# The opening of a two-layer decoder trunk: four projection tiles interleaved in chunks of k, and an identity made on the chip

## The chip, the core and the metric

The kernel runs on one core of a Trainium2 chip. A core has TensorE (matmuls; in the profile PE, and PEld for its weight loads), VectorE (DVE), ScalarE (ACT), GpSimd (POOL) and SyncE (SP, which here only issues loads and stores), each with an instruction stream of its own that runs in order. They meet through semaphores. Working memory is SBUF, with 128 partitions; matmuls write to PSUM, of which this kernel uses eight banks of 128 x 512 float32. DMA engines move data between the chip's memory and SBUF. The metric is the time of one execution on the device in microseconds, lower is better.

## The reference

Two layers of a trunk for 256 tokens of width 1024, all float32. The part that the change touches is the first feed-forward step of the first layer:

```python
D_MODEL, SEQ, DEPTH, D_FF = 1024, 256, 2, 2816

def swiglu(x, w_gate, w_up, w_down):
    return (jax.nn.silu(x @ w_gate) * (x @ w_up)) @ w_down

h = x
for l in range(DEPTH):
    h = h + 0.5 * swiglu(rms_norm(h, ffn1_norm[l]), ffn1_w_gate[l], ffn1_w_up[l], ffn1_w_down[l])
    h = h + hybrid_mixer(rms_norm(h, mix_norm[l]), ...)     # three attention groups, then w_out
    h = h + 0.5 * swiglu(rms_norm(h, ffn2_norm[l]), ffn2_w_gate[l], ffn2_w_up[l], ffn2_w_down[l])
```

`rms_norm` divides a token by the root of its mean square and multiplies by a gain for each column.

## The kernel before

**Split numbers.** Every float32 operand of a large matmul is split into a high part (the value rounded to the fast matmul type) and a low part (the rest). A product is then high x high + high x low + low x high. `norm.x` (tile `xhl`) holds both parts of the normalized, transposed activations side by side, 8 k tiles of 128 with 2 x 256 columns; `norm.h` and `norm.l` are its halves. A projection tile of 128 output columns is a wide pass (weights' high part against 512 columns, 8 matmuls) and a narrow pass (low part against 256 columns, 8 matmuls). The two halves of the PSUM bank are then added by `summed`: ScalarE copies one half to SBUF, VectorE adds the other.

**Weights.** The class `Weights` streams all weights of the program through five raw buffers of 1 MB (`RAW_BUFS`) and eight pairs of split buffers (`wh`, `wl`). A raw tile holds two units (for the feed-forward step two tiles of 128 columns with all 8 k). `high` casts a unit on ScalarE (line 117), `low` subtracts on VectorE (line 121), `take` hands a unit to the matmuls, and `pump` does one cast and one subtraction ahead of need, as long as fewer than seven units lie ready. When both units of a raw tile are split, `issue` starts the next load, on SyncE's queue. Loads, units and matmuls all keep one order, which `add_ffn` writes down when the program is built. All instruction orders are as written in the program: nothing is moved by a scheduler.

**The feed-forward loop.** `ffn` runs over 22 tiles f of 128 hidden columns. For each it needs a gate and an up projection, `gated` and `silu` (VectorE, with a tanh on ScalarE), and `hidden`, which multiplies by up, splits the result (`hh` on ScalarE, then a `W.pump`, then `hl` on VectorE) and keeps it for the down projection, which lags by four tiles (`DOWN_LAG`). The projections use four PSUM banks under the tag `gu`, in turn. From f = 6 on in the first step, and everywhere else, gate and up run as a `Pair`: for even f both wide passes, then both narrow ones; for odd f the narrow ones first (`swapped`). In the first step the tiles f < 6 (`PAIR_FROM`) run singly, first gate, then up, by `proj`; the third gate tile uses one of the other four banks (`acc`).

**The opening.** The identity for TensorE's transposes comes from memory, on ScalarE's queue (line 184), as do the gains of the first norm. SyncE loads x in four quarters of 256 columns, with the first gate tile's two k halves between them, then the first up tile, then the second halves of those two raw tiles. TensorE runs warm-up matmuls on a tile of ones (`WARM` = 7, twice). `norm.turn` transposes two k tiles of x, `first_norm` writes their high part on ScalarE (line 320) and their low part on VectorE (line 323), and `gate` starts the first gate tile on them while the next quarter arrives, in three passes of 256 columns. For this first tile the cast is on ScalarE (line 1150) and the subtraction on GpSimd (line 1151), in two halves. Then come the first up tile, the second gate tile, the sums of squares, and so on. The norm's factor (`sums`, `broadcast`) is applied after the projection, in `gated` and `silu`.

Of the kernel before, what the change touches and what calls it, by code (L numbers as in the profile page):

```python
# [18 lines left out]
P = 128  # L19
# [18 lines left out]
WARM = 7  # L38
PAIR_FROM = 6
# [102 lines left out]
def kernel(ctx: ExitStack, tc: tile.TileContext, x, ffn1_norm, ffn1_w_gate, ffn1_w_up, ffn1_w_down,  # L142
# [25 lines left out]
    cst = cp.tile([P, 640], F32, name="cst")  # L168
# [15 lines left out]
    nc.scalar.dma_start(cst[:, 0:P], const[:, 0:P])  # L184
# [18 lines left out]
    def add_ffn(wg, wu, wd, first=False):  # L203
# [3 lines left out]
        def half(kind, i):  # L207
            j = i // 2
            if (kind, j) not in rid:
                if kind == "d":  # L210
                    rid[kind, j] = W.add_raw((2, D), [(np.s_[:], dsrc[:, 2 * j:2 * j + 2, :])])
                else:
                    src = gsrc if kind == "g" else usrc
                    src = src[:, :, 256 * j:256 * j + 256]
                    cuts = [np.s_[:]]
                    if first and j == 0:
                        cuts = [np.s_[:, :, 0:P], np.s_[:, :, P:2 * P]]
                        if kind == "g":
                            cuts[:1] = [np.s_[:, 0:4, 0:P], np.s_[:, 4:8, 0:P]]
                    rid[kind, j] = W.add_raw((KT, 256), [(c, src[c]) for c in cuts])  # L220
            o = i % 2
            if kind == "d":
                W.add_unit(rid[kind, j], lambda r, o=o: r[:, o:o + 1, :], D, 1)
            else:
                W.add_unit(rid[kind, j], lambda r, o=o: r[:, :, o * P:(o + 1) * P], D, KT)

        for f in range(NF):
            half("g", f)
            if not first or f >= PAIR_FROM:
                half("u", f)  # L230
# [4 lines left out]
            if first and f < PAIR_FROM:  # L235
                half("u", f)
# [35 lines left out]
    nc.sync.dma_start(cst[:, P:], const[:, P:])  # L272
# [7 lines left out]
    ident = cst[:, 0:128]  # L280
    tri = cst[:, 128:256]
    future = cst[:, 256:384]
    cs = cst[:, 384:640].rearrange("p (t c) -> p t c", t=2)
# [90 lines left out]
    def ffn(norm, nxt, aside=None, g0=None):  # L374
# [23 lines left out]
        def proj(between=None, after=0, tag="gu"):  # L398


            w = W.take()
            ps = bank(tag).rearrange("p (a b) -> p a b", a=2)
            for k in range(KT):
                mm(ps, w[0][:, k], norm.x[:, k], k == 0, False)
            for k in range(KT):
                mm(ps[:, 0], w[1][:, k], norm.h[:, k], False, k == KT - 1)
                if between and k == after:
                    between()
            return ps

        class Pair:


            def __init__(self):
                self.ws = [W.take() for _ in range(2)]
                self.ps = [bank("gu").rearrange("p (a b) -> p a b", a=2) for _ in range(2)]

            def wide(self, ks):
                for w, ps in zip(self.ws, self.ps):
                    for k in ks:  # L420
                        mm(ps, w[0][:, k], norm.x[:, k], k == 0, False)

            def narrow(self, ks):
                for w, ps in zip(self.ws, self.ps):
                    for k in ks:
                        mm(ps[:, 0], w[1][:, k], norm.h[:, k], False, k == KT - 1)

            def swapped(self, between):

                for w, ps in zip(self.ws, self.ps):  # L430
                    for k in range(KT):
                        mm(ps[:, 0], w[1][:, k], norm.h[:, k], k == 0, False)
                between()
                for w, ps in zip(self.ws, self.ps):
                    for k in range(KT):
                        mm(ps, w[0][:, k], norm.x[:, k], False, k == KT - 1)
# [37 lines left out]
        first = g0 is not None  # L474
        early = {}
        if first:
            u0 = proj()
            g1 = proj(norm.sums, 6)
            W.pump()
            W.low()  # L480
            g0 = summed(g0)
            u1 = proj(norm.broadcast, 6)
            W.pump(2)
            early[2] = proj(tag="acc")
        else:
            lo, hi = range(KT // 2), range(KT // 2, KT)
# [5 lines left out]
            W.pump()  # L492
            norm.sums()
            (g0, u0), (g1, u1) = p0.both(hi), p1.ps
            W.pump()
            g0, u0 = summed(g0), summed(u0)
            W.pump()
            p1.wide(hi)
            norm.broadcast()
            p1.narrow(hi)  # L500
            W.pump()
        early[1] = g1
# [3 lines left out]
        hidden(0, t_, th, summed(u0) if first else u0)  # L506
        acc = [bank("acc") for _ in range(4)]
        for f in range(1, NF):
            last = f == NF - 1
            paired = not first or f >= PAIR_FROM  # L510
            inside = paired and f > 1

# [4 lines left out]
            if not paired:  # L517
                g, u = summed(early[f] if f in early else proj()), u1 if f == 1 else None
            else:
                if f == 1:  # L520
                    g, u = g1, u1
                elif f % 2:
                    g, u = Pair().swapped(lagging)
                else:
                    p = Pair()
                    p.wide(range(KT))
                    lagging()
                    p.narrow(range(KT))
                    g, u = p.ps
                if last:  # L530
                    W.pump()
                g = summed(g)
                if not last:
                    u = summed(u)
# [4 lines left out]
            else:  # L539
                W.pump()  # L540
                if not inside:
# [4 lines left out]
            hidden(f, t_, th, u if paired and not last else summed(u or proj()), 3 if last else 1)  # L546
# [580 lines left out]
    for i in range(WARM):  # L1127
        mm(warm[:, :P], ones, ones, i == 0, i == WARM - 1)
    norm = Norm(0, 0)
    src, wh, wl = W.high_tiles()  # L1130
    g0 = bank("gu").rearrange("p (a b) -> p a b", a=2)
    xT = []

    def turn_x(mp):
        xT.append(norm.turn(mp))

    def gate(w, xs, ks):
        for k in ks:
            mm(g0[:, int(xs is norm.l)], w[:, k], xs[:, k], w is wh and xs is norm.h and k == 0,
               xs is norm.l and k == KT - 1)  # L1140

    def first_norm(mp):
        for i in range(2):
            norm.high(2 * mp + i, xT[mp][:, i])
        for i in range(2):
            norm.low(2 * mp + i, xT[mp][:, i])

    def split_gate(hf):
        ks = slice(4 * hf, 4 * hf + 4)
        A.copy(wh[:, ks], src[:, ks])  # L1150
        G.tensor_tensor(wl[:, ks], src[:, ks], wh[:, ks].bitcast(F32), op=ALU.subtract)

    turn_x(0)
    turn_gains(0)
    for i in range(WARM):
        mm(warm[:, P:2 * P], ones, ones, False, i == WARM - 1)
    split_gate(0)
    first_norm(0)
    turn_x(1)
    split_gate(1)  # L1160
    for mp in range(4):
        ks = range(2 * mp, 2 * mp + 2)
        gate(wh, norm.h, ks)
        if mp < 2:
            turn_x(mp + 2)
        if mp > 0:
            gate(wl, norm.h, range(4) if mp == 1 else ks)
        gate(wh, norm.l, ks)
        if mp < 3:
            first_norm(mp + 1)  # L1170
    W.low_done()
    W.take()
    W.high()
    W.low()
    W.high()
    W.low()
    for c in range(2):
        for t in range(2):
            norm.squares(t, c)
    W.high()  # L1180
    W.low()
    for l in range(DEPTH):
        norm = ffn(norm, lambda: Norm(1, l), lambda: before_mixer(l), g0 if l == 0 else None)
# [37 lines left out]
```

## Time and profile before

| | |
|---|---|
| median of 3 runs | 1039.59 us (1039.53 to 1040.01) |
| profiled execution | 1040.75 us, of which the span from first to last instruction is 1039.0 us |
| TensorE busy | 1032.8 us, 99% of the span, 5659 matmuls |
| VectorE, ScalarE, GpSimd busy | 78%, 57%, 14% |
| loaded | 179.67 MB, 174 GB/s over the span |
| granted TensorE clock | 1.000 of full speed |

Times in the rows are microseconds from the span's start. A row of the timeline reads: start, duration, engine, line, operation, output <- inputs, shape, count of merged instructions, and in brackets the idle time before it and what ended that. Matmuls overlap in their pipeline, so the distance between starts, not the duration, is what one costs. "SPq" and "ACTq" are issues of loads. Each landing time is counted from the start of the issue.

### The profile page before, as it was taken

Reading aid. Unit: us, or ns where it says so; the run is one execution under the profiler, and the core shown is the slowest. Engines: PE = TensorE matmul, PEld = TensorE weight load, DVE = VectorE, ACT = ScalarE, POOL = GpSimd, SP = SyncE. Lnnn points to the kernel's source line nnn. Section 1 sums busy time; section 2 is a strip of 40 time slices with the busy share of each in tenths; the row PEclk is TensorE's granted clock in tenths of the full one; section 3 lists DMA queues with packets and bytes.
Section 4 is the critical chain, followed back from the end, with each engine's and each line's share of the span. In section 5 each row is a group of like instructions: output and inputs, shape, how many; then the busy total and the mean of one; then the engine's idle time right before and its main releaser. Section 6 shows DMA issues by size and latency. Waiting matters only on the chain.

```text
span 1039.0 us, 15103 instructions
## 1 busy us (share of the span) xinstructions
PE 1032.8 (99%) x5659; PEld 899.7 (87%) x5659; DVE 807.9 (78%) x1536; ACT 593.8 (57%) x1047; POOL 142.3 (14%) x173
## 2 busy tenths in 40 slices
PE   8999999999999999999999999999999999999998
PEld 8888888898888888888888888888988988888887
DVE  4988778789876877777778777787898768777776
ACT  6655555667754655555465555557667546555552
POOL 1003000167700000000000110002765000000000
PEclk9999999999999999999999999999999999999999
DMA  9764646555441354746645564655455214555631
GB/s 292 249 226 150 240 152 226 168 184 193 144 144 42 122 205 160 242 146 220 203 163 175 198 207 158 243 177 180 163 185 180 82 61 157 189 201 165 231 133 41
DMA packets 130905, 181.70 MB, mean 175 GB/s; under 512 B 7008, under 2 KB 104720, under 8 KB 130832
## 3 DMA queue, kind: packets, MB, share of 16 engines
q1 hardware_dynamic: 130656, 180.65, 51.8%
q8 instruction: 45, 0.74, 0.3%
q14 instruction: 28, 0.23, 0.1%
q10 hardware_dynamic: 176, 0.07, 0.0%
HBM read 179.67 MB, written 1.05 MB: 174 GB/s over the span
## 4 chain that ended last, share of the span: by engine, by line
PE 99%; DMA 1%; SPq 0%; issue 0%; ACT 0%; DVE 0%; ACTq 0%
PE ps_gu L296 66%; PE ps_acc L296 30%; PE ps_acc L331 1%; PE ps_gu L980 1%; PE ps_gu L1082 1%; DMA trunk<-in_x_dram 1%; PE ps_acc L681 0%; PE ps_acc L980 0%; PE ps_gu L1013 0%; SPq L91 0%; SPq L188 0%; PE ps_acc L357 0%; PE ps_acc L1013 0%; ACT pT L982 0%; DVE trunk L370 0%
## 5 line engine op out<-in xcount | busy, mean ns | idle before, releaser
L121 DVE TENSOR_TENSOR wl<-raw,wh 128x1024 fp32r<-128x1024 f32 (+2 forms) x343 | 416.8, 1220 | 28.7 <-ACT wh L117 28.4
L117 ACT CAST wh<-raw 128x1024 fp32r<-128x1024 f32 (+2 forms) x343 | 345.5, 1036 | 6.2 <-PE ps_gu L296 4.9
L296 PE MATMUL ps_gu<-xhl,wh 128*128 128x512 f32 (+1 forms) x1408 | 329.4, 388 | 0.0
L296 PEld LDWEIGHTS ps_gu<-xhl,wh 128*128 128x128 f32 x1408 | 262.0, 188 | 52.9
L296 PEld LDWEIGHTS ps_gu<-xhl,wl 128*128 128x128 f32 x1400 | 175.8, 191 | 4.2
L296 PE MATMUL ps_gu<-xhl,wl 128*128 128x256 f32 x1400 | 178.9, 283 | 0.0
L296 PE MATMUL ps_gu<-wh,xhl 128*128 128x512 f32 (+2 forms) x512 | 158.5, 379 | 0.0
L448 DVE TENSOR_TENSOR tmp<-ps_gu,tmp 128x256 f32<-128x256 f32 x175 | 72.8, 422 | 105.2 <-ACT tmp L447 105.0
L296 PE MATMUL ps_acc<-wh,hh 128*128 128x512 f32 (+1 forms) x352 | 137.2, 390 | 0.0
L296 PE MATMUL ps_acc<-wl,hh 128*128 128x512 f32 (+1 forms) x352 | 137.0, 389 | 0.0
L296 PE MATMUL ps_acc<-wh,hl 128*128 128x512 f32 (+1 forms) x352 | 136.5, 388 | 0.0
L447 ACT COPY tmp<-ps_gu 128x256 f32<-128x256 f32 x175 | 63.4, 370 | 91.1 <-PE ps_gu L296 91.0
L296 PEld LDWEIGHTS ps_gu<-wh,xhl 128*128 128x128 f32 x512 | 94.8, 188 | 14.5
L462 ACT CAST hh<-tmp 128x256 fp32r<-128x256 f32 x80 | 32.6, 407 | 120.0 <-DVE tmp L459 120.0
L296 PE MATMUL ps_gu<-wl,xhl 128*128 128x512 f32 (+2 forms) x256 | 95.7, 374 | 0.0
L454 ACT ACTIVATE tmp<-tmp 128x256 f32<-128x256 f32 x88 | 36.9, 419 | 82.0 <-DVE tmp L452 81.7
L307 POOL TENSOR_TENSOR y_n<-msq,minus_half 128x2 f32<-128x2 f32 x6 | 6.8, 1138 | 534.6 <-DVE msq L306 534.6
L296 PEld LDWEIGHTS ps_acc<-wh,hl 128*128 128x128 f32 x352 | 66.1, 188 | 13.9
L296 PEld LDWEIGHTS ps_acc<-wh,hh 128*128 128x128 f32 x352 | 66.3, 188 | 12.5
L296 PEld LDWEIGHTS ps_acc<-wl,hh 128*128 128x128 f32 x352 | 66.3, 188 | 12.1
L296 PEld LDWEIGHTS ps_gu<-wl,xhl 128*128 128x128 f32 x256 | 48.2, 188 | 6.6
L472 DVE TENSOR_TENSOR tmp<-tmp,rb 128x256 f32<-128x256 f32 x88 | 37.5, 427 | 3.0
(221 smaller groups left out, 995.4 us busy)
## 6 DMA issues: line engine op xcount, KB each, us to landing
raw<-in_ffn_w_down_dram SPq DMA_DIRECT2D x44, 1024.0 KB, 5.0
raw<-in_ffn_w_gate_dram SPq DMA_DIRECT2D x43, 1024.0 KB, 7.0
raw<-in_ffn_w_up_dram SPq DMA_DIRECT2D x43, 1024.0 KB, 7.5
raw<-in_w_in_dram SPq DMA_DIRECT2D x24, 1024.0 KB, 5.0
raw<-in_w_out_dram SPq DMA_DIRECT2D x8, 1024.0 KB, 4.8
raw<-in_w_in_dram SPq DMA_DIRECT2D x4, 768.0 KB, 4.7
raw<-in_w_in_dram SPq DMA_DIRECT2D x4, 656.0 KB, 4.1
trunk<-in_x_dram SPq DMA_DIRECT2D x4, 256.0 KB, 5.4
```

The costliest lines, as they stand in the source:

```text
L117: self.nc.scalar.copy(hv, src)
L121: (engine or self.nc.vector).tensor_tensor(lv, self.srcs[self.n_low], hv.bitcast(F32), op=ALU.subtract)
L296: T.matmul(o, l, r, start=start, stop=stop, skip_group_check=True)
L307: G.tensor_tensor(y, dst, minus_half[:, :n], op=ALU.pow)
L331: T.transpose(ps[:, i, t * P:(t + 1) * P], trunk[:, t, (2 * mp + i) * P:(2 * mp + i + 1) * P], ident)
L447: A.copy(o, ps[:, 1])
L448: V.tensor_tensor(o, ps[:, 0], o, op=ALU.add)
L454: A.activation(th, t_, AF.Tanh, scale=0.5)
L462: (V.tensor_copy if late else A.copy)(hh, t_)
L472: V.tensor_tensor(t_, t_, norm.rb, op=ALU.mult)
L980: T.transpose(b[:, j * P:(j + 1) * P], pj[i][:, j * P:(j + 1) * P], ident)
L1082: T.transpose(b[:66, i * S + t * P:i * S + (t + 1) * P], src[t][:, 2 * hp_ + i, :], ident)
```

## The change

- The first two raw tiles (gate and up of f = 0 and 1) are loaded in three pieces each, by k: 0-1, 2-3, 4-7, all 256 columns at a time. SyncE's order is x quarter 0, gate 0-1, up 0-1, x quarter 1, gate 2-3, up 2-3, x quarters 2 and 3, gate 4-7, up 4-7, and then the third and fourth raw tile in column halves. A unit of the first two raw tiles is now four k with 256 columns.
- A new function `opening` runs the gate and up tiles of f = 0 and 1 together, in four PSUM banks. For each quarter of x it transposes, splits, and runs the wide pass of all four tiles on that k, with the narrow passes behind. In it GpSimd casts the first two pieces of both raw tiles and the last piece of the gate's, VectorE subtracts for the gate's first pieces and GpSimd for the up's. The rest of these four tiles then runs through the code that the later steps use.
- All f run as `Pair`, and the unit order is gate, up for every f. `proj` and `PAIR_FROM` are gone.
- The identity is made on GpSimd from the tile of ones. The constants are loaded in one piece, without an identity, where the rest of them was loaded before.
- The gains are transposed ahead of x, and the warm-up is 6 matmuls ahead of these transposes and 3 behind the first ones.

```diff
-WARM = 7
-PAIR_FROM = 6
+WARM = 6
+BRIDGE = 3
...
-    nc.scalar.dma_start(cst[:, 0:P], const[:, 0:P])
+    G.affine_select(out=ident, in_=ones, pattern=[[-1, P]], compare_op=ALU.is_equal, fill=0.0, base=0,
+                    channel_multiplier=1)
...
-                    if first and j == 0:
-                        cuts = [np.s_[:, :, 0:P], np.s_[:, :, P:2 * P]]
-                        if kind == "g":
-                            cuts[:1] = [np.s_[:, 0:4, 0:P], np.s_[:, 4:8, 0:P]]
+                    if first and j < 2:
+                        cuts = ([np.s_[:, 0:2], np.s_[:, 2:4], np.s_[:, 4:8]],
+                                [np.s_[:, :, 0:P], np.s_[:, :, P:2 * P]])[j]
...
+            elif first and j == 0:
+                W.add_unit(rid[kind, j], lambda r, o=o: r[:, 4 * o:4 * o + 4], D, 4)
...
         for f in range(NF):
             half("g", f)
-            if not first or f >= PAIR_FROM:
-                half("u", f)
+            half("u", f)
...
-            if first and f < PAIR_FROM:
-                half("u", f)
...
-    W.by_hand = 2
-    W.n_raw_done -= RAW_BUFS - 2
+    W.by_hand = 4
+    W.n_raw_done -= RAW_BUFS - 4
     W.issue()
-    for mp in range(1, 4):
-        if mp < 3:
-            W.load(0, mp - 1)
+    for m in range(2):
+        if m:
+            load_x(m)
+        for i in range(2):
+            W.load(i, m)
+    for mp in range(2, 4):
         load_x(mp)
-    W.load(1, 0)
-    W.load(0, 2)
-    W.load(1, 1)
-    W.n_raw_done += RAW_BUFS - 2
+    for i in range(2):
+        W.load(i, 2)
+    for m in range(2):
+        for i in range(2):
+            W.load(2 + i, m)
+    W.n_raw_done += RAW_BUFS - 4
     W.issue()
...
+        def opening():
+            low = [W.high_tiles() for _ in range(2)]
+            p0, p1 = (Pair([[[v[:, k, f * P:(f + 1) * P] for k in range(4)] for v in (h, l)] for _, h, l in low])
+                      for f in range(2))
+            def highs(m):
+                ks = slice(2 * m, 2 * m + 2)
+                for src, h, _ in low:
+                    G.tensor_copy(h[:, ks], src[:, ks])
+            def lows(m):
+                ks = slice(2 * m, 2 * m + 2)
+                for E, (src, h, l) in zip((V, G), low):
+                    E.tensor_tensor(l[:, ks], src[:, ks], h[:, ks].bitcast(F32), op=ALU.subtract)
+            def wide(k):
+                for i in range(2):
+                    for p in (p0, p1):
+                        mm(p.ps[i], p.ws[i][0][k], norm.x[:, k], k == 0, False)
+            def narrow(k):
+                for i in range(2):
+                    for p in (p0, p1):
+                        mm(p.ps[i][:, 0], p.ws[i][1][k], norm.h[:, k], False, False)
...
+            xT = norm.turn(0)
+            warm_up(BRIDGE)
+            highs(0)
+            parts(0, xT)
+            lows(0)
+            wide(0)
+            xT = norm.turn(1)
+            wide(1)
+            narrow(0)
+            narrow(1)
+            highs(1)
+            parts(1, xT)
+            lows(1)
+            for _ in range(2):
+                W.low_done()
+                W.take()
+            squares(0)
+            xT = norm.turn(2)
+            wide(2)
+            parts(2, xT)
+            xT = norm.turn(3)
+            wide(3)
+            parts(3, xT)
+            narrow(2)
+            narrow(3)
+            src, h, _ = W.high_tiles()
+            G.tensor_copy(h, src)
+            W.high()
+            W.low()
+            W.low()
+            squares(1)
...
         if first:
-            u0 = proj()
-            g1 = proj(norm.sums, 6)
-            W.pump()
-            W.low()
-            g0 = summed(g0)
-            u1 = proj(norm.broadcast, 6)
-            W.pump(2)
-            early[2] = proj(tag="acc")
+            p0, p1 = opening()
         else:
             p0, p1 = Pair(), Pair()
             p0.wide(lo)
             norm.half(1)
             p0.narrow(lo)
             p1.both(lo)
+        W.pump()
+        norm.sums()
+        (g0, u0), (g1, u1) = p0.both(hi), p1.ps
+        W.pump()
+        g0, u0 = summed(g0), summed(u0)
+        W.pump()
+        p1.wide(hi)
+        norm.broadcast()
+        p1.narrow(hi)
+        W.pump()
```

More of the change, by code (lines that the diff above doesn't have):

```diff
@@ L505, in ffn @@
         silu(t_, th)
-        hidden(0, t_, th, summed(u0) if first else u0)
+        hidden(0, t_, th, u0)
         acc = [bank("acc") for _ in range(4)]
@@ L540, in ffn @@
                 W.pump()
-                if not inside:
+                if f == 1:
                     lagging()
@@ L545, in ffn @@
             silu(t_, th)
-            hidden(f, t_, th, u if paired and not last else summed(u or proj()), 3 if last else 1)
+            hidden(f, t_, th, summed(u) if last else u, 3 if last else 1)
             if f == 8 and aside:
```

154 lines of the change are left out of this document (48 added, 106 removed).

## The prediction

> **What bounds the kernel now.** I read the page's busy shares first, then TensorE's waits over the whole run, then its timeline around the opening, and then the loads and the ScalarE/VectorE/GpSimd rows that feed it.
>
> ```profile
> span 1039.0 us, 15103 instructions
> PE 1032.8 (99%) x5659; PEld 899.7 (87%) x5659; DVE 807.9 (78%) x1536; ACT 593.8 (57%) x1047; POOL 142.3 (14%) x173
> ...
> PE ps_acc L331 <- DMA trunk<-in_x_dram: 1.7, 1, 1.7
> PE ps_gu L296 <- POOL minus_half L183: 1.0, 1, 1.0
> PE ps_gu L296 <- ACT pT L982: 0.2, 1, 0.2
> ...
> 0.97 3.35 PE L296 MATMUL ps_gu<-ones 128*128 128x128 f32 x14 [0.97 <-POOL minus_half L183]
> 4.32 0.70 PE L331 MATMUL ps_acc<-cst,trunk 128*128 128x128 f32 x4
> 4.95 0.23 PE L177 MATMUL ps_gu<-cst,tmp 16*128 16x16 f32 x1
> 5.11 1.83 PE L296 MATMUL ps_gu<-ones 128*128 128x128 f32 x14
> 6.77 0.60 PE L331 MATMUL ps_acc<-cst,trunk 128*128 128x128 f32 x4
> 7.13 0.48 PE L296 MATMUL ps_gu<-xhl,wh 128*128 128x256 f32 x2
> 9.36 0.66 PE L331 MATMUL ps_acc<-cst,trunk 128*128 128x128 f32 x4 [1.74 <-DMA trunk<-in_x_dram]
> 15.79 2.00 PE L296 MATMUL ps_gu<-xhl,wh 128*128 128x512 f32 x8
> 17.63 1.12 PE L296 MATMUL ps_gu<-xhl,wl 128*128 128x256 f32 x8
> 18.59 2.00 PE L296 MATMUL ps_gu<-xhl,wh 128*128 128x512 f32 x8
> 27.19 2.00 PE L296 MATMUL ps_gu<-xhl,wh 128*128 128x512 f32 x8
> ```
>
> TensorE has three waits in all. After 9.36 it only once waits again, for 0.2 us, so from there the time is a pile of matmuls with no slack. The opening can only help or harm by the moment at which that pile is resumed. One projection tile (eight k, a wide 512-column and a narrow 256-column pass) costs 18.59 - 15.79 = 2.80 us. Up to 9.36 the useful work was eight transposes (0.35 to 0.4 us for four: 6.77 to 7.13, and 9.36 to the next row at 9.77), the gains and two matmuls: about 1.2 us. So some 8.1 us of the start are idle or warm-up. That is all that can be won, less the 4 us until x lands.
>
> A yardstick follows. In order, six projections (gate and up of f = 0, 1, 2) are done when the seventh starts at **27.19**. The changed kernel does the same six before its seventh (the gate of f = 3, on `swapped`), and the later matmul list is the same in amount. The change in time is therefore the start of that seventh projection minus 27.19, unless a new wait comes later.
>
> **The change part by part.** *The identity.* The const load on ScalarE's queue goes and GpSimd makes the identity. The program also holds a library-load instruction on GpSimd ahead of its first work that is not a memset: before that is L1151, after it is the select, so it moves to the front of the path.
>
> ```profile
> 1.15 0.15 POOL L601 MEMSET eighth<- 128x64 f32 x1
> 5.72 1.27 POOL L1151 TENSOR_TENSOR wl<-raw,wh 128x512 fp32r<-128x512 f32 x1 [4.41 <-ACT wh L1150]
> 9.35 1.29 POOL L1151 TENSOR_TENSOR wl<-raw,wh 128x512 fp32r<-128x512 f32 x1 [2.36 <-ACT wh L1150]
> ...
> 0.72 0.20 POOL L181 MEMSET ones<- 128x128 f32 x1 [0.29 <-POOLq L1209]
> ...
> DMA to landing us min/median/max: 3.5/3.5/3.5
> 1.21 0.48 SPq L91 DMA_DIRECT2D raw<-in_ffn_w_gate_dram  x1
> DMA to landing us min/median/max: 3.8/3.8/3.8
> ```
>
> The load lies somewhere in the 4.41 us in which GpSimd was idle before 5.72, so it costs 0 to 4.4 us, and the identity is ready between 1.2 and 5.6 us. x's first quarter, issued at 0.72, landed 3.5 us later at 4.2, and the first gate piece, second in the queue before and after, at 1.21 + 3.8 = 5.0. If the load is short, the identity is early; at worst the transposes slip by 1.4 us. I take a small value and keep 1.4 us as the bound of this part. It is covered, because the seventh projection waits for something later (below). The Trainium skill ("GPSIMD Engine Reference", section "Instruction dispatch") says that the first call to a freshly loaded kernel pays about 6 us; the trace disagrees, since the first such call here ran 4.4 us after the memsets at its ordinary 1.27 us. By that page the identity would be there at 7.2 and the sum below would rise by at most 0.2 us, since GpSimd's work would end some 2.6 us later.
>
> *Four tiles together.* By rows, wide(k) is four wide matmuls (2.00 / 8 each, or 0.92 us at their spacing), so half of the four tiles (k 0 to 3) is 5.6 us of work on 512 KB of x and 1 MB of weights. It replaces nothing: it is the same matmuls sooner, and the first gate tile's three 256-column passes become 512 + 256 (gain below 0.1 us). Warm-up shrinks from 7 + 7 to 6 + 3 matmuls, in time that is idle anyway. GpSimd now does five casts, four of 128x512 and one of 128x1024, and two subtractions (1.28 us each). No row shows a GpSimd cast; it reads less than the subtraction (1.28 us) and writes more than the 0.20 us memset of 128x128 scaled to 512 columns (0.6 us): 0.6 to 1.28 us each, double for the large one. At 1.28 GpSimd, starting on the gate piece at 5.0, needs 4 x 1.28 + 2 x 1.28 + 2.56 = 10.2 us and is done at 15.2; at 0.6 it follows the loads. With the second half of the four tiles (5.6 us) plus broadcast behind 15.2, the four tiles end at about 21.1 and f = 2 (2 x 2.80) at 26.7; at the short price about 26.0. So TensorE itself would be ready for the seventh projection at 26.0 to 26.7: **0.5 to 1.2 us early**.
>
> *What is late next.* The seventh projection writes the PSUM bank of f = 1's gate, which `summed` (ScalarE copy, VectorE add) must first empty. In the changed order, on ScalarE's queue, `hidden(0)` pumps a weight cast ahead of that copy, and by the new unit order (gate and up alternating from the start) it is the cast of f = 4's up weights: the sixth raw tile, the first for which a buffer has to come free. ScalarE works in order, so the copy stands behind a transfer. Before, the cast in that place belonged to weights of an earlier raw tile.
>
> ```profile
> raw<-in_ffn_w_gate_dram SPq DMA_DIRECT2D x43, 1024.0 KB, 7.0
> ...
> trunk<-in_x_dram SPq DMA_DIRECT2D x4, 256.0 KB, 5.4
> ...
> cst<-in_const_dram SPq DMA_DIRECT2D x1, 256.0 KB, 9.3
> ...
> 20.80 0.39 SPq L91 DMA_DIRECT2D raw<-in_ffn_w_down_dram  x1
> DMA to landing us min/median/max: 7.3/7.3/7.3
> 21.29 0.41 SPq L91 DMA_DIRECT2D raw<-in_ffn_w_up_dram  x1
> DMA to landing us min/median/max: 9.5/9.5/9.5
> 2.28 0.47 SPq L91 DMA_DIRECT2D raw<-in_ffn_w_gate_dram  x1
> DMA to landing us min/median/max: 6.4/6.4/6.4
> ...
> 10.00:20.00 10.00, 10.00 (x66) 9.04 (x65) 6.94 (x12) 8.39 (x18) 1.33 (x2) 1.00 0.97 291
> 20.00:30.00 10.00, 10.00 (x62) 8.90 (x61) 7.82 (x14) 5.54 (x10) 0.00 (x0) 1.00 1.06 374
> ```
>
> The loads are in one queue and the queue is full: the DMA engines are 97 to 106% busy from 10 to 30 us (last rows, last two columns: share and GB/s). So landing follows the bytes queued ahead. Before, the first down tile had landed at 20.80 + 7.3 = 28.1, with 7,520 KB queued up to its end (x 1024, five raw tiles 5120, const 64 + 256, small ones 32, itself 1024). In the changed order the up tile of f = 4 comes in that place, with 64 KB less: **27.9** if the stream runs as before (1024 KB per 2.7 us there: 21.29 + 9.5 = 30.8 is the next). The other end: from 8.68 (2.28 + 6.4, 1,096 KB) the remaining 6,360 KB at the 374 GB/s of the last row take 17.4 us, **26.1**. The first two raw tiles now come in 1 KB rows where before had 512-byte rows, and the next two the other way round: the same mixture, so I stay nearer to the 27.9 and take 27.2.
>
> ```profile
> 27.66 1.05 ACT L117 CAST wh<-raw 128x1024 fp32r<-128x1024 f32 x1
> 28.61 0.36 ACT L447 COPY tmp<-ps_gu 128x256 f32<-128x256 f32 x1
> ...
> 29.00 0.42 DVE L448 TENSOR_TENSOR tmp<-ps_gu,tmp 128x256 f32<-128x256 f32 x1 [0.22 <-ACT tmp L447]
> ...
> 34.30 0.42 DVE L448 TENSOR_TENSOR tmp<-ps_acc,tmp 128x256 f32<-128x256 f32 x1 [0.22 <-ACT tmp L447]
> ```
>
> Behind the landing come cast, copy and add: 28.61 - 27.66 + 29.00 - 28.61 + 0.42 = 1.76, with the hand-overs about 1.85 us. Seventh projection: 27.2 + 1.85 = 29.05, against 27.19: **+1.9 us**; at the ends 27.95 (+0.8) and 29.75 (+2.6). TensorE's readiness at 26.0 to 26.7 is hidden by it, and so are the identity, the casts and the early x. What TensorE wins by starting sooner goes into this one wait of 2.4 to 3 us. After it VectorE's time for a tile, (34.30 - 29.00) / 2 = 2.65 us, fits TensorE's 2.80, as before, so I cost later waits at nothing; the later loads are then asked for 1.9 us later, too, which keeps them covered.
>
> The profiled execution took 1040.75 us, 1.75 over its span and 1.2 over the median of 1039.59. I carry the difference over to the median: 1039.6 + 1.9 = **1041.5**.
>
> **The rivals.** *The loads are in time* (one piece at 374 GB/s from 5 us on, landing before 25.3): seventh projection at 26.0 to 27.2, 1038.4 to 1039.6. For it: nothing queued early is in 512-byte rows. Against it: 291 GB/s between 10 and 20 us in a full queue.
>
> *No wait at all in the opening* (loads early and GpSimd at its short price, so that only x's landing and the transposes hold TensorE): 8.1 us of idle shrink to about 6, 1037.5. Against it: nine hand-overs between four engines in 15 us.
>
> *GpSimd becomes the bound* (the other side): if a cast takes longer than the subtraction, or VectorE's subtractions beside it slow both, GpSimd ends at 5.0 + 6c + 2.56, and the seventh projection starts 11.4 us later. It decides from 29.05 on, c = 1.7 us; at c = 2.0 it is 31.0, +3.8: 1043.4. Against it: both L1151 rows took 1.27 to 1.29 with VectorE at work on the same tiles' neighbours.
>
> *The clock falls in the gap.* TensorE then stands still for 2.4 to 3 us. The opening rows show a slow state (14 instructions in 3.35 us, later 14 in 1.83) and that a gap of 1.74 us does not bring it back; a longer one is not in this trace. If it does, about 3.4 us of work run at half speed: +1.7, 1043.2. The Trainium skill ("TensorE: Matmul & The Clock Gate", Part 1) puts that at a whole idle window of about 3.4 us; the gap is shorter, so by it the chance is small.
>
> *The identity is later than the const load was* is possible up to 5.6 us, as worked out, and changes nothing but the early idle time.
>
> **How the numbers follow.** Cases: the wait on ScalarE 0.60; loads in time 0.20; no wait 0.05; GpSimd 0.10; clock 0.05. A measurement of this kernel can tell about 0.2%, 2.1 us. The first case spans +0.8 to +2.6: 0.27 of it lies above 2.1, 0.33 below; with GpSimd and clock, slower has 0.42. Loads in time give 0.17 to same and 0.03 to faster, no wait 0.05: same 0.50, faster 0.08. The range leaves out 0.05 at the low end and the worst of the last two cases: 1038.3 to 1043.4; the likeliest case alone has 1040.4 to 1042.2.
>
> **What would show it.** In the changed profile: the first wide matmul at 6.3 to 7.5 us; the four tiles done at 20 to 21 (before: 21.5); then one wait of TensorE of 2 to 3 us before f = 3's first narrow matmul, at about 29, released by VectorE's add, with ScalarE idle before the cast of the sixth raw tile on a gate or up load that landed at about 27. I am wrong if that load lands before 25, if there is no wait between 24 and 31, or if GpSimd's casts take over 1.3 us and TensorE's waits name it.

## The result

The changed kernel took 1042.6 us (median of 9 runs, 1041.5 to 1043.88), the kernel before 1039.85 us beside it (9 runs, 1039.53 to 1040.18): the ratio is 1.0025, with an interval of 1.0016 to 1.0034. The profiled execution of the changed kernel took 1043.26 us with a span of 1041.2; TensorE is busy for 99% of it, as before. The four longest of its five waits over the whole run (the fifth is the one of 0.2 us that the kernel before has too):

```profile
PE ps_gu L300 <- DVE tmp L439: 2.1, 1, 2.1
PE ps_gu L300 <- POOL minus_half L184: 1.0, 1, 1.0
PE ps_gu L300 <- DVE xhl L327: 0.9, 1, 0.9
PE ps_gu L300 <- POOL wh L474: 0.7, 1, 0.7
```

The wait for x's third quarter (1.7 us before) is gone; a new one of 2.1 us stands in its place, and VectorE's add (L439, `summed`) releases it. (Those of 0.9 and 0.7 us lie in the opening, before the first wide matmuls.) The timeline around it, with the load that stands at its start and that load's landing:

```profile
6.31 0.70 PE L300 MATMUL ps_gu<-xhl,wh 128*128 128x512 f32 x2 [0.87 <-DVE xhl L327]
20.24 3.82 PE L300 MATMUL ps_gu<-xhl,wh 128*128 128x512 f32 x16
23.90 2.07 PE L300 MATMUL ps_gu<-xhl,wl 128*128 128x256 f32 x16
28.07 3.63 PE L300 MATMUL ps_gu<-xhl,wl 128*128 128x256 f32 x16 [2.10 <-DVE tmp L439]
31.54 0.63 PE L300 MATMUL ps_gu<-xhl,wh 128*128 128x512 f32 x2
...
19.27 0.39 SPq L91 DMA_DIRECT2D raw<-in_ffn_w_up_dram  x1
DMA to landing us min/median/max: 6.9/6.9/6.9
26.24 1.04 ACT L117 CAST wh<-raw 128x1024 fp32r<-128x1024 f32 x1 [2.15 <-DMA raw<-in_ffn_w_up_dram]
27.19 0.64 ACT L438 COPY tmp<-ps_gu 128x256 f32<-128x256 f32 x2
27.59 0.76 DVE L439 TENSOR_TENSOR tmp<-ps_gu,tmp 128x256 f32<-128x256 f32 x2 [2.36 <-ACT tmp L438]
```

The four tiles are done at 20.24, f = 2 at about 25.8. Then TensorE stands still: ScalarE waits 2.15 us for the sixth raw tile, f = 1's copies stand behind that cast, and f = 3's gate waits for the bank that they empty. It starts at 28.07. Then its sixteen narrow matmuls take 31.54 - 28.07 = 3.47 us. The same view of busy time by stretches (TensorE's busy time and count, granted clock as a share of full speed, busy share and GB/s of the DMA engines) says why:

```profile
26.00:28.00 2.00, 0.00 (x0) 0.99 1.02 402
28.00:30.00 2.00, 1.93 (x9) 0.50 1.08 386
30.00:31.50 1.50, 1.50 (x9) 0.54 1.09 386
31.50:33.00 1.50, 1.50 (x9) 1.00 0.96 341
```

Behind the gap the granted clock is 0.50 until about 31.5. By the clock that each run lists, this happened in five of the nine runs (mean clock 0.998, median span 1041.4); in the other four it was 1.000 (median span 1040.05). So there are two terms: a wait, and in more than half of the executions a spell of half speed behind it.

### The profile page after: what moved, and what is told of

Same layout as the page of the kernel before. It is cut to its first block, busy times and chain, and to the rows that moved or that the text cites. A ratio compares the mean times of both kernels' runs of the same rounds, so it can differ in the third digit from the quotient of the medians.

```text
span 1041.2 us, 15082 instructions
## 1 busy us (share of the span) xinstructions
PE 1033.2 (99%) x5641; PEld 899.2 (86%) x5641; DVE 807.7 (78%) x1537; ACT 591.7 (57%) x1043; POOL 145.8 (14%) x179
## 4 chain that ended last, share of the span: by engine, by line
PE 97%; SPq 1%; DMA 1%; issue 0%; ACT 0%; DVE 0%; ACTq 0%
PE ps_gu L300 64%; PE ps_acc L300 29%; DMA raw<-in_ffn_w_up_dram 1%; SPq L91 1%; PE ps_acc L335 1%; PE ps_gu L1029 1%; PE ps_gu L1131 1%; PE ps_acc L730 0%; PE ps_acc L1029 0%; PE ps_gu L1062 0%; SPq L277 0%; PE ps_acc L1062 0%; SPq L174 0%; PE ps_acc L361 0%; ACT pT L1031 0%
## 5 line engine op out<-in xcount | busy, mean ns | idle before, releaser
L300 PE MATMUL ps_gu<-xhl,wh 128*128 128x512 f32 x1408 | 330.5, 390 | 1.5 <-DVE xhl L327 0.9
L439 DVE TENSOR_TENSOR tmp<-ps_gu,tmp 128x256 f32<-128x256 f32 x176 | 72.9, 422 | 112.9 <-ACT tmp L438 112.7
L324 ACT ACTIVATE xhl<-ps_acc,gT 128x256 fp32r<-128x256 f32 x48 | 19.0, 474 | 41.6 <-PE ps_acc L335 41.6
```

The lines of the kernel that those rows point to most:

```text
L300: T.matmul(o, l, r, start=start, stop=stop, skip_group_check=True)
L324: A.activation(self.h[:, m], src, AF.Copy, scale=gT[:, self.col + m:self.col + m + 1])
L439: V.tensor_tensor(o, ps[:, 0], o, op=ALU.add)
```

## The experiments

Four kernels ran beside each other with 35 runs of the kernel before (median 1039.83), then four more with 33 (1039.69) on another chip, then three single executions with a profile on the first chip. In all of them the start of the seventh projection (the gate of f = 3) is read from the timeline, as in the prediction.

**1. The cast behind the copies.** ScalarE's order alone is changed: `hidden(0)` pumps no cast in the first step, `hidden(1)` two.

```diff
-        hidden(0, t_, th, u0)
+        hidden(0, t_, th, u0, 0 if first else 1)
...
-            hidden(f, t_, th, summed(u) if last else u, 3 if last else 1)
+            hidden(f, t_, th, summed(u) if last else u, 3 if last else 2 if first and f == 1 else 1)
```

> The changed kernel, with one cast moved: hidden(0) of the first step pumps nothing, and hidden(1) pumps twice, so that the cast of f = 4's up weights stands behind f = 1's two copies on ScalarE. Theory W (the wait in ScalarE's queue, and the clock that falls in its gap, are the whole loss): TensorE goes from f = 2 straight to f = 3 at about 26.0, no wait named VectorE L439, no stretch at half clock; the whole is 27.19 - 26.0 = 1.2 us under before, span about 1037.8, time 1038.4 to 1038.8. Rival L (TensorE is simply ahead of the loads, and would wait for that tile one step later): a wait of 1 to 2 us reappears between 26 and 33, and the time stays at 1040 to 1042. Rival O (the opening itself, with GpSimd's casts, costs more than before's): nothing below 1039.8.

Measured: 1039.08 us (11 runs), ratio to before 0.9998 (0.999 to 1.0007), no run below clock 1.000. A second set (below) gave 1039.22. The medians lie a little above the expected 1038.4 to 1038.8, and by its interval the kernel cannot be told from the kernel before; by spans it has a median of 1037.0 in both sets, against 1038.0 and 1037.9. TensorE's row runs through, ScalarE's copies (rows of the second set) stand ahead of the cast:

```profile
23.27 4.00 PE L300 MATMUL ps_gu<-xhl,wl 128*128 128x256 f32 x32
...
23.54 0.64 ACT L438 COPY tmp<-ps_gu 128x256 f32<-128x256 f32 x2
25.51 1.04 ACT L117 CAST wh<-raw 128x1024 fp32r<-128x1024 f32 x1
```

The thirty-two narrow matmuls of f = 2 and f = 3 are one row: the gap is gone, f = 3 starts at about 25.2, sooner than the 26.0 expected. One cast moved in ScalarE's queue takes away the whole loss against the kernel before. That settles the wait's mechanism.

**2. The constants behind the weights.** The loads of the constants, two gains and the forget bias (280 KB) are issued behind the opening, so that the sixth raw tile has less ahead of it.

```diff
-    nc.sync.dma_start(cst, const)
-    load_gains(1, mix_norm, nc.sync)
-    load_gains(2, ffn2_norm, nc.sync)
...
             p0, p1 = opening()
+            late_loads()
```

> The changed kernel, with the constants (256 KB), two gain loads and the forget bias issued behind the opening's loads, so that 280 KB less are ahead of f = 4's up weights in the queue. Theory W with its price by bytes: at 380 GB/s that tile lands 0.75 us sooner, at about 25.4, and f = 3 starts at about 27.3 instead of 28.07, after a wait of 1.35 us; if the clock falls only in longer gaps, the half-clock stretch goes too: 1039.7 to 1040.3, against 1042.6. If it still falls: 1041.3 to 1041.9. Rival (the landing is set by when the load is issued, 19.27, not by the bytes ahead of it): landing and wait unchanged, 1041.5 to 1043.5.

Measured: 1041.5 (11 runs), ratio 1.0018 (1.0009 to 1.0027); four runs with a lower clock. In its profile the load of the sixth raw tile was issued at 16.40 instead of 19.27 and landed at the same time:

```profile
DMA to landing us min/median/max: 9.7/9.7/9.7
26.13 1.04 ACT L117 CAST wh<-raw 128x1024 fp32r<-128x1024 f32 x1 [1.30 <-DMA raw<-in_ffn_w_up_dram]
27.96 2.17 PE L302 MATMUL ps_gu<-xhl,wl 128*128 128x256 f32 x16 [2.43 <-DVE tmp L441]
```

16.40 + 9.7 = 26.1, against 19.27 + 6.9 = 26.2 with 280 KB more ahead. In this execution the pricing of a landing by the bytes queued ahead of it fails. From 15 to 20 us the engines moved 329 GB/s where the changed kernel has 362, and 393 against 348 from 20 to 26; that what is queued behind takes part of the rate is one reading of this, and not shown.

The runs say something else than the trace. The profiled execution has the longest span (1039.6) of the seven at full clock; the other six lie at 1038.2 to 1039.4, all below the four of the changed kernel at full clock (1039.8 to 1040.3, taken in another set). With 1011.6 us behind the start of f = 3, as in this trace (1039.6 - 27.96), the median span of 1038.9 puts that start at about 27.3, an estimate, and just where the pricing by bytes expected it. So whether less ahead brings the landing forward stays open. In this profiled execution the clock did not fall, although the gap was 2.43 us: the sixteen matmuls took 2.0 us. In the four runs where it fell, the median span is about 2.4 us above that of the other seven, more than the 1.5 us of the changed kernel's profile; none of the four was profiled, and where the rest lies is open.

**3 and 7. Work in the gap.** Filler matmuls of a tile of ones against itself, written to a bank that nothing uses yet, stand behind f = 2: n is 7 in the first kernel, 13 in the second (the trace counts each as two). The wait for the cast stays.

```diff
                 g, u = p.ps
+                if first and f == 2:
+                    for i in range(n):
+                        mm(acc[0][:, :P], ones, ones, i == 0, i == n - 1)
```

> The changed kernel, with seven warm-up matmuls on the tile of ones behind f = 2 (1.8 us of TensorE's gap filled, into a bank that the down projection overwrites later). The wait for the copy stays. Theory W (of the loss 0.9 us is the wait and 1.5 us the clock): f = 3 starts at 28.0 to 28.2 as in the changed kernel, its first sixteen narrow matmuls take 1.9 us instead of 3.5, mean clock 1.000 in every run, time 1040.3 to 1041.0. Rival (the clock has nothing to do with the gap, or the slow narrow matmuls come from operands that arrive late): the sixteen still take 3.5 us and the time stays at 1041.5 to 1043.5.

> As the third experiment, with 13 filler matmuls of 128 columns instead of 7 after f = 2, so that TensorE has no idle time left before f = 3 (13 at about 0.15 us, against a gap of 2.1 us). The wait for the cast of the sixth raw tile is kept. Theory (two separate terms: the wait, +0.9 us, and in some executions a fall of the clock in the gap, +1.5 us): no execution shows a mean clock below 1.000, the spread of the runs closes, 1040.6 to 1041.4, and f = 3 starts at 27.9 to 28.1 as before. Rival (the lower mean clock comes from somewhere else than the gap): as many executions at 0.998 as with 7 fillers, 2 in 11, or more.

Measured with 7: 1041.37 (11 runs), ratio 1.0022 (1.0013 to 1.0031), a gap of 0.89 us left in the profile, two of eleven runs with a lower clock (0.998). With 13: 1041.57 (11 runs), ratio 1.002 (1.0011 to 1.0029), and no run at 0.998 (one at 0.999, as four of the 68 of the kernel before, and no longer than the rest). Both medians lie somewhat above what was expected, 1040.3 to 1041.0 and 1040.6 to 1041.4, and with 7 a clock of 1.000 in every run had been expected. The timeline and the stretches with 13:

```profile
23.42 2.07 PE L300 MATMUL ps_gu<-xhl,wl 128*128 128x256 f32 x16
25.33 3.06 PE L300 MATMUL ps_acc<-ones 128*128 128x128 f32 x26
28.18 2.17 PE L300 MATMUL ps_gu<-xhl,wl 128*128 128x256 f32 x16
...
28.00:30.00 2.00, 2.00 (x19) 1.00 1.09 386
30.00:31.50 1.50, 1.50 (x9) 1.00 1.09 388
```

f = 3 starts as late as in the changed kernel (28.18 against 28.07), but at full clock. So the two terms are separate: 13 fillers leave the wait, the clock does not fall, and nine of eleven spans lie at 1039.7 to 1040.1. The other two, 1041.5 and 1041.6, are as long as with a fall, but their clock is 1.000; like one run with 7 fillers (1041.4) they were not profiled and stay open.

That the fall comes with the gap rests on more than this pair, since the two kernels ran on different chips. On the first chip 0.998 stands in four of eleven and four of twelve runs with a gap (experiments 2 and 4), and in none of eleven without one (experiment 1). In all, none of the 68 runs of the kernel before and of the 44 without a gap (experiments 1, 5, 7 and 8) shows it. How much a fall costs is less clear: with 7 fillers the two runs are 2.6 and 5.0 us longer in span than the median of the others.

**4. The identity loaded again.** The changed kernel with the identity from memory, on ScalarE's queue.

```diff
-    G.affine_select(out=ident, in_=ones, pattern=[[-1, P]], compare_op=ALU.is_equal, fill=0.0, base=0,
-                    channel_multiplier=1)
+    nc.scalar.dma_start(ident, const[:, 0:P])
```

> The changed kernel, with the identity loaded from memory again on ScalarE's queue, ahead of the gains, and not made by GpSimd: that part of the change undone alone. Theory W: the transposes wait for x (landed at 3.8 in the changed kernel) and the gains anyway; the gains land 0.5 us later and 64 KB more are ahead of every weight, 0.2 us; this goes into the wait at f = 3, so 0 to +0.4 us against the changed kernel, 1041.6 to 1044. Rival (the identity on the chip is a gain of its own, about 1 us): 1043.5 to 1044.5. Rival (GpSimd's select delays its casts): 0.3 us or more faster than the changed kernel.

Measured: 1041.49 (12 runs), ratio 1.0023 (1.0013 to 1.0033), four runs with a lower clock (0.998).

```profile
4.95 0.20 PE L178 MATMUL ps_gu<-ident,tmp 16*128 16x16 f32 x1 [1.05 <-DMA tmp<-in_ffn_norm_dram]
20.26 3.82 PE L299 MATMUL ps_gu<-xhl,wh 128*128 128x512 f32 x16
25.64 1.04 ACT L117 CAST wh<-raw 128x1024 fp32r<-128x1024 f32 x1 [1.52 <-DMA raw<-in_ffn_w_up_dram]
27.47 2.18 PE L299 MATMUL ps_gu<-xhl,wl 128*128 128x256 f32 x16 [1.48 <-DVE tmp L438]
```

The opening starts 1 us later (4.95 against 3.90 with the identity made on the chip), because the gains now stand behind the identity on ScalarE's queue. The four tiles do not notice: they are done at 20.26, against 20.24 in the changed kernel's profile (19.59 in its other one, below). The gap at f = 3 is smaller for another reason: the sixth raw tile landed at 25.6 (18.18 + 7.4) instead of 26.2. From 5 to 10 us the loads ran at 363 GB/s here, and at 309 and 313 in the changed kernel's two profiles; why stays open. So the identity made on the chip is no gain in this kernel. The time lies below all that Theory W gave, and by its number the second rival came true: the median span of the eight runs without a fall is 1039.25, 0.8 us less than the changed kernel's 1040.05. But that rival's mechanism is not in the trace, since in the changed kernel the select ends at 1.38 and GpSimd's first cast then waits for its load until 4.57. The four runs with a fall are about 3.3 us longer by the median span, and were not profiled either.

**6. The identity alone.** The kernel before with GpSimd's select in place of the identity's load, and nothing else.

> The kernel before with only the identity made by GpSimd instead of loaded; the tiles, the order and the loads are as before. If the opening of before is bound by x's second pair of quarters, as its wait of 1.74 us at 9.36 says, the identity gives only what 64 KB less ahead of x are worth, 64 KB at 240 to 340 GB/s, 0.2 to 0.3 us: 1039.3 to 1039.8, no change that can be told. If the library load on GpSimd cost something on the path (rival, up to 1.4 us): 1040 to 1041. The first transposes should start at about 4.1 to 4.3 instead of 4.32.

Measured: 1039.99 (11 runs), ratio 1.0001 (0.9992 to 1.0009): no difference that can be told. The median is 0.2 us above the expected range, next to the rival's 1040, but the rival's delay is not in the trace: the first transposes start at 4.19, as expected.

```profile
8.33 0.66 PE L332 MATMUL ps_acc<-cst,trunk 128*128 128x128 f32 x4 [0.54 <-DMA trunk<-in_x_dram]
26.16 2.00 PE L297 MATMUL ps_gu<-xhl,wh 128*128 128x512 f32 x8
```

Here the profile misled: the wait for x is 0.54 instead of 1.74, the seventh projection starts at 26.16 instead of 27.19, and yet the median is no better. So the yardstick itself had to be looked at.

**9 and 10. The kernel before, two more profiled executions.**

> The kernel before, unchanged, in one more profiled execution. The yardstick of the prediction, the seventh projection at 27.19, came from one execution with a span of 1039.0, while 68 executions beside the experiments had spans of 1037.1 to 1039.8 with medians of 1037.9 and 1038.0. Theory (the wait for x's third quarter, 1.74 us there, and the load rate of 291 GB/s between 10 and 20 us belong to that execution, and so does 1 us of the yardstick): span 1037.4 to 1038.4, a wait for x of 0.3 to 1.0 us, seventh projection at 25.8 to 26.6. Rival (the opening is always the same, and the difference lies elsewhere): wait of 1.5 to 1.9, seventh projection at 27.0 to 27.3.

> The same once more, as a second sample of the yardstick: span 1037.4 to 1038.4, seventh projection at 25.8 to 26.6, against the rival's 27.0 to 27.3.

Measured: 1041.47 and 1039.38, spans 1039.7 and 1037.6. The timeline of the first (two rows) and of the second (three):

```profile
5.87 3.36 PE L296 MATMUL ps_gu<-ones 128*128 128x128 f32 x14
27.91 2.00 PE L296 MATMUL ps_gu<-xhl,wh 128*128 128x512 f32 x8
...
5.02 1.83 PE L296 MATMUL ps_gu<-ones 128*128 128x128 f32 x14
8.03 0.66 PE L331 MATMUL ps_acc<-cst,trunk 128*128 128x128 f32 x4 [0.50 <-DMA trunk<-in_x_dram]
25.85 2.00 PE L296 MATMUL ps_gu<-xhl,wh 128*128 128x512 f32 x8
```

The same kernel starts its seventh projection at 25.85, 27.19 or 27.91. The second hit what was expected, the first neither theory: there x was hardly waited for (0.31 us), but the second batch of warm-up matmuls (seven, which the trace counts as fourteen) took 3.36 us instead of 1.83. Span less start of the seventh projection is 1011.75, 1011.81 and 1011.79. The identity alone gives 1011.84, the changed order at full clock 1011.4 to 1011.7 (experiments 1 to 5 and 7), and the changed kernel 1041.2 - 28.07 = 1013.13, the 1.5 us of the clock above them. So the yardstick's rule (what comes behind this start is always as long) holds to 0.1 us in the order of before and to 0.3 us in the changed one; its value does not hold.

**11. The changed kernel, one more profiled execution.**

> The changed kernel, unchanged, in one more profiled execution. If the clock fell in this one too, the sixteen narrow matmuls of f = 3 take about 3.5 us and the span is near 1041.4; if it did not, they take 2.0 to 2.2 us, with the same gap of about 2 us before them, and the span is near 1040.0. Either way f = 3 starts at 27.8 to 28.2, behind the cast of the sixth raw tile, on a load landed at about 26.0 to 26.2.

Measured: 1042.94, span 1041.2, mean clock 0.998.

```profile
19.59 3.82 PE L300 MATMUL ps_gu<-xhl,wh 128*128 128x512 f32 x16
28.03 3.31 PE L300 MATMUL ps_gu<-xhl,wl 128*128 128x256 f32 x16 [2.71 <-DVE tmp L439]
```

The four tiles were 0.65 us sooner (19.59 against 20.24), the gap that much longer (2.71 against 2.10), f = 3 where it was (28.03 against 28.07), and the clock fell again (sixteen matmuls in 3.1 us). What TensorE wins ahead of this wait goes into it.

**5 and 8. The cast behind the copies once more, without and with another order of the first two k tiles.** Experiment 8 is experiment 1 again. Experiment 5 also takes the first two k tiles in another order: high and low part of each at once, the gate's wide matmuls of both ahead of the up's.

```diff
-            wide(0)
+            wide(0, [0])
+            wide(1, [0])
             xT = norm.turn(1)
-            wide(1)
+            wide(0, [1])
+            wide(1, [1])
...
+                if mp == 0:
+                    for i in range(2):
+                        norm.high(i, ps[:, i])
+                        norm.low(i, ps[:, i])
+                    return
```

> The cast moved behind f = 1's copies as in the first experiment, and the opening's first two k tiles taken in another order: both gate weights first, then the up weights, and x's first two k tiles split one after the other (high, low, high, low). In the first experiment TensorE stood still for 0.87 us before the first wide matmul (behind ScalarE's two casts and VectorE's first subtraction, 4.89 to 6.2) and about 0.7 us before the up weights. Theory (the time is the start of the seventh projection, and nothing else waits up to there): first wide matmul at about 5.9, the seventh projection 0.4 to 0.8 us sooner than in the first experiment, 1038.0 to 1038.6 by the median. Rival (the loads bound the opening: each later piece of x and of the weights is taken as it lands): the start is sooner, but TensorE waits for x's third quarter at about 9.5 to 10 or for the second half of the weights by about the same amount, and the time stays at 1038.9 to 1039.2.

> The kernel of the first experiment once more (the cast of the sixth raw tile behind f = 1's copies), beside more runs of the kernel before, since its eleven runs fell into two groups (six at spans of 1036.8 to 1037.0, five at 1037.7 to 1038.8), all at clock 1.000. Theory: below before by 0.5 to 1.5 us, 1038.3 to 1039.3 by the median, no run with a lower clock. Rival (the first result was the chance of one opening): 1039.5 to 1040.2, no different from before.

Measured: with both edits 1038.74 (11 runs, 1038.17 to 1039.7), ratio 0.999 (0.9981 to 0.9999); the cast behind the copies alone, again, 1039.22 (11 runs), ratio 0.9997 (0.9988 to 1.0006). Both came out below the kernel before, the first by an interval that just leaves out 1, the second by one that does not. TensorE's waits with both edits, and three of its first rows:

```profile
PE ps_gu L300 <- POOL minus_half L184: 1.0, 1, 1.0
PE ps_gu L300 <- ACT pT L1038: 0.2, 1, 0.2
...
4.12 1.11 PE L335 MATMUL ps_acc<-ident,trunk 128*128 128x128 f32 x4
5.02 1.49 PE L300 MATMUL ps_gu<-ones 128*128 128x128 f32 x6
6.41 1.67 PE L300 MATMUL ps_gu<-xhl,wh 128*128 128x512 f32 x4
```

Only the wait at the very start and one of 0.2 us are left. The expected earlier start (5.9) did not come: here the transposes and the bridge of warm-up matmuls ran slowly (1.11 and 1.49 us; 0.66 and 0.83 in the changed kernel's profile) and lasted to 6.41. Nor did the seventh projection start sooner: about 25.5 here, 25.2 and 25.3 with only the cast moved. The time, 1038.74, lies between the ranges of the theory and of the rival. By spans the second edit gives nothing in the middle: all three sets have a median of 1037.0. What differs is the spread. All eleven spans with both edits lie at 1036.5 to 1037.1, while of the 22 with only the cast moved seven lie at 1037.7 to 1038.8, all at mean clock 1.000. Five of these seven ran on the other chip, and beside each other it is two of eleven against none, so this may be chance. What happens in the seven was not caught in a profile and stays open.

## Why the prediction came out as it did

**The wait (right).** Its place, its releaser, the cause (the sixth raw tile's cast ahead of f = 1's copies on ScalarE) and the chain behind the landing (1.85 us predicted; 28.07 - 26.2 = 1.9 measured) were as written, and experiment 1 shows the cause by taking it away. TensorE's own readiness (26.0 to 26.7 predicted, about 25.8 measured) went into the gap, and so did an early start; the two executions of the changed kernel show that (experiment 11).

**The landing (a term too large by 1 us).** The step "I stay nearer to the 27.9 and take 27.2" failed: the tile landed at 26.2, at the other end (26.1). The rate of 291 GB/s between 10 and 20 us, on which the 27.9 rested, was not repeated: the changed kernel has 362, and the kernel before 375 and 367 in its two other executions (the last two columns are the busy share and GB/s of the DMA engines):

```profile
10.00:20.00 10.00, 10.00 (x68) 9.09 (x66) 7.02 (x12) 8.84 (x19) 0.51 (x1) 1.00 1.10 375
10.00:20.00 10.00, 10.00 (x63) 8.98 (x62) 6.69 (x11) 7.19 (x15) 0.69 (x1) 1.00 1.09 367
```

In these two the load in that place of the queue, the first down tile, landed at 26.1 and 26.2 (17.73 + 8.4 and 19.70 + 6.5), not at 28.1. One execution's rate was taken for the kernel's. How far the bytes ahead set the landing, experiment 2 leaves open.

**The yardstick (too late by 1 us).** 27.19 belonged to one execution. With the median of 1039.85 and 1.75 us around the span the usual start is 1039.85 - 1.75 - 1011.8 = 26.3, an estimate. So the wait is worth 28.07 - 26.3 = 1.8 us, not 28.07 - 27.19 = 0.9. Landing and yardstick were off by about the same, and cancelled: +1.9 was predicted, and the four runs at full clock have a median of 1041.8, 1.96 above before. That part of the forecast came out right for a reason that is half luck. Carrying the difference over to the median, as the prediction did, does not cure a yardstick from a slow opening.

**The clock (the rival with 0.05).** It came about in five of nine runs, and in both profiled executions, at +1.5 us in the profile (1.7 predicted). That is what lifts the median from 1041.8 to 1042.6, above the likeliest case's 1040.4 to 1042.2, and the ratio over the 0.2% at which the prediction drew its line; 0.50 stood below it, 0.42 above. The step that failed is the weight. It rested on a gap of 1.74 us that had left the clock alone, and on the rule of the Trainium skill ("TensorE: Matmul & The Clock Gate", Part 1), by which the clock falls after a whole idle window of about 3.4 us. Gaps of 2.10 and 2.71 us were followed by half speed here, so the measurement disagrees with that length. The same page says that the window runs freely against the program; that some executions fall and others not, and that a gap of 2.43 us in experiment 2 was not followed by it, would fit with that, but no run here shows the window itself.

**GpSimd and the identity (right, at the cheap ends).** The identity was ready at 1.38, so the library load costs nothing on the path (the select starts at 1.09, row below), and the 6 us that the prediction quoted and doubted are not there within the span. The casts took 0.61 us, the lower bound; GpSimd as the bound did not come about. But they are not always cheap:

```profile
1.09 0.29 POOL L185 TENSOR_SCALAR_AFFINE_SELECT ident<-ones 128x128 f32<-128x128 f32 x1
4.57 0.61 POOL L474 CAST wh<-raw 128x512 fp32r<-128x512 f32 x1 [2.85 <-DMA raw<-in_ffn_w_gate_dram]
6.47 0.68 DVE L479 TENSOR_TENSOR wl<-raw,wh 128x512 fp32r<-128x512 f32 x1
6.57 1.06 POOL L474 CAST wh<-raw 128x512 fp32r<-128x512 f32 x1 [1.39 <-DMA raw<-in_ffn_w_up_dram]
10.19 1.29 POOL L479 TENSOR_TENSOR wl<-raw,wh 128x512 fp32r<-128x512 f32 x1
10.55 1.48 DVE L479 TENSOR_TENSOR wl<-raw,wh 128x512 fp32r<-128x512 f32 x1
```

Beside VectorE's subtraction (6.47) the second cast takes 1.06 instead of 0.61, and beside GpSimd's subtraction (10.19) VectorE's takes 1.48 instead of 0.68. In both pairs the later one ends about 0.5 us after the earlier one has ended (7.63 against 7.15, 12.03 against 11.48), a little less than its own length, so it looks as if it waited for the other and did not run beside it more slowly. The prediction had GpSimd's subtractions at "1.27 to 1.29 with VectorE at work", and they did stay at 1.28 and 1.29; it was VectorE that paid. The Trainium skill ("GPSIMD Engine Reference", section "Key points") says that GpSimd contends with VectorE instructions that have two inputs in SBUF, as these subtractions do; the trace agrees.

**No wait, loads in time.** Neither rival came about in the changed kernel. Experiment 1 comes near to the first of them: f = 3 starts at about 25.2, where that rival had it (27.19 - 2.1), but the time is 1039.1, not 1037.5, mostly because the yardstick was 1 us too late.

## What to carry to other kernels

A step that starts sooner is worth nothing as long as an engine that works in order has, ahead of its hand-over, an instruction that waits for a load: look in the new order for the first cast of a late buffer, and put it behind the copies that free a bank. A gap on TensorE can cost more than its length, since half speed may follow; where a wait cannot be removed, matmuls of no use in it kept the clock here (no fall in eleven runs), though they do not shorten the wait. And a yardstick that is read from the opening of one execution needs a second execution of the same kernel: here it moved by 2 us, as much as the effect looked for.

## What the runs showed of the hardware that was not expected

- Half speed followed gaps of 2.10 and 2.71 us, for 3 to 3.5 us, but not one of 2.43, and not in every execution. Mean clock 0.998 stands in 5 of 9 runs of the changed kernel, 4 of 11 and 4 of 12 in experiments 2 and 4 (profiled gaps of 2.43 and 1.48 us), 2 of 11 with 0.89 us left, none of 11 with none.
- The slow spell of TensorE at the start does not show in the granted clock: the column reads 1.00 from 0 to 10 us in both profiles of the kernel before, of experiments 9 and 10, although the second batch of equal warm-up matmuls took 3.36 us in the one and 1.83 in the other. Its end varies from one execution to the next, between about 4 and 9 us.
- In the one profile of it, a load issued 2.9 us sooner, with 280 KB less ahead of it, landed 0.1 us sooner (26.1 against 26.2). Over five executions with the same loads (the changed kernel twice, experiments 1, 3 and 7) this landing lies at 25.6 to 26.3, so one profile does not settle it.
- VectorE's subtraction of 128x512 took 0.68 us where it started first, and 1.48 where GpSimd's had started 0.36 us ahead of it; GpSimd's own time stayed at 1.29.
